# A margin on the ready time in the emitter that interleaves projection pieces with dense matmuls

## The chip, the cores and the metric

The kernel runs on one core of one Trainium2 chip. The metric is the device time of one execution in microseconds. The time of a kernel is the median of its runs; the kernel before was run three times.

## The reference

Two layers of an encoder trunk on 2048 rows of 1024 channels. The even layer runs a gated DeltaNet and an RWKV-7 mixer side by side, the odd layer a Hyena operator. Each begins with one wide input projection. Cut to what matters here:

```python
def even_mixer(x, w_in, ...):
    proj = x @ w_in
    dn_qkv, dn_ab, dn_gate, rk_in, rk_gate = jnp.split(proj, EVEN_SPLITS, axis=-1)
    qkv = jax.nn.silu(dwconv_centred(dn_qkv, dn_conv)).astype(f32)
    q = l2_normalize(q.reshape(bsz, seq, DN_HEADS, DN_DK))
    k = l2_normalize(k.reshape(bsz, seq, DN_HEADS, DN_DK))
    ...
    s = bidir_token_shift(rk_in, rk_mu)
    a = jax.nn.sigmoid(rk_a0 + a_d @ rk_a2)
    kk = l2_normalize(heads(k * rk_k_k))
    k = k * (1.0 + (a - 1.0) * rk_k_a)
    ...

def odd_mixer(x, w_in, ...):
    proj = x @ w_in
    xv, gate = jnp.split(proj, [(HY_ORDER + 1) * HY_WIDTH], axis=-1)
    xv = dwconv_centred(xv, conv_w, conv_b)
    filt = hyena_filters(...)
    ...

def reference(x, p, ...):
    h = x
    for i in range(DEPTH):
        mix = even_mixer(...) if i % 2 == 0 else odd_mixer(...)
        h = layer_norm(DEEPNORM_ALPHA * h + mix @ w_out[i], ln_g[i], ln_b[i])
        e = rms_norm(p[i] @ ple_w[i], ple_norm[i])
        h = h + jax.nn.sigmoid(h @ ple_gate[i]) * e
    return h
```

## The kernel before

The stages run one after another: the even layer's projections (`phase_a`), its two scans, the layer's tail, the odd layer's projections (`phase_d`), the Hyena convolutions, the tail. Both projections are done by `project` (line 1003).

`project` works through a list of jobs. A job is one block of 128 output channels (34 jobs in `phase_a`, 32 in `phase_d`). Its dense part is four blocks, one for each quarter of 512 rows. A block is 24 matmuls of 128x512 into one PSUM bank (8 slices of 128 input channels, and for each the three products of the high and low parts of x and of the weights, `xh`, `xl`, `wh`, `wl`), and ScalarE then copies the bank into the job's row buffer `pb`. There are two such buffers. When all four blocks of a job have been emitted, its four pieces may start, one for each quarter: what happens to these channels behind the projection.

The pieces of `phase_a` come in rounds of eight jobs: `delta(0)` (q), `rwkv(0)`, `delta(1)` (k), a gate, `delta(2)` (v), `rwkv(1)` (k), a gate, `rwkv(2)` (v); there are four rounds behind two small jobs. A piece is a Python generator. It emits some instructions, yields the tile that its next step reads, and goes on when it is chosen again. A `delta` piece for q or k convolves and applies SiLU (`th`, the tile u), and yields it; transposes it on TensorE, copies it to `tm`, squares it on GpSimd (`sq`), and yields that; sums it on VectorE (`ss`, `rs`), raises it to a power on GpSimd (`rr`), and yields that; scales `tm` on VectorE, and yields that; transposes `tm` back on TensorE, copies it out (`cm`) and stores it. The steps from the first transposition on are `normalised` (line 838) and `to_channels`. An `rwkv(1)` piece has one more step, a small matmul with `ad`, before the same normalisation (`kx` in the place of u). A `delta(2)` piece waits once, for u. The pieces of `phase_d` yield no tile, but for those of the filter network `hyena_mlp`, which runs beside them.

The order of emission is made by `weave` (line 1119). Its threads are, in this order, `hyena_mlp` where there is one, four threads of pieces (`post(k)` takes quarter k of every job, one job after another), and `gemm`, which emits the dense blocks. It keeps clocks of the engines by the costs in `Ahead.cost` (line 320) and the time at which each tile is there, `have`. At each turn it takes the first thread whose ready time is not past the clock of TensorE, otherwise the one with the least ready time. After a block `gemm` yields an empty tuple and is ready at once. Before it emits job n, `gemm` yields None, that is, it passes, until all pieces of the jobs up to n-2 are done (`while min(done[:n - 1]) < 4`, line 1096). A yielded tile sets the thread's ready time:

```python
pick = next((t for t in cand if t[1] <= m.clk["P"]), None) or min(cand, key=lambda t: t[1])
m.now = max(pick[1], m.clk["P"])
...
pick[1] = max([m.have.get(x.name, 0.0) for x in r], default=0.0)
```

The scans use `weave` too (line 1687), and then fix the order of every instruction by dependencies of their own. In the projections nothing is fixed: the order of emission is a priority, and the compiler's pass orders each engine's instructions by it and by when it expects their operands.

Of the kernel before, what the change touches and what calls it, by code (L numbers as in the profile page):

```python
# [143 lines left out]
class Ahead:  # L144
# [203 lines left out]
    @staticmethod  # L348
    def beside(out):

        return out.offset // out.ap[0][0] % P >= 64
# [315 lines left out]
class Trunk:  # L667
# [335 lines left out]
    def project(self, src, xh, xl, wp, t2, ps, bank, jobs, pad, beside=None, first=None, tbs=(0, 1, 2, 3), early=None):  # L1003
# [5 lines left out]
        st = {"g": 0}  # L1009

        def fetch(n):
            if n >= NJ:
                return
            r = wp.tile([P, KT, P], F32, name=self.n("wr"), tag="wraw", bufs=1)
            o = 0
            for ap in jobs[n][0]:
                m = ap.shape[1]
                nc.sync.dma_start(r[:, :, o:o + m], ap.rearrange("(k p) m -> p k m", p=P))
                o += m
            raw[n] = r, o  # L1020

        def split(n):
            if n >= NJ:
                return
            r, m = raw.pop(n)
            wh = wp.tile([P, KT, P], F32R, name=self.n("wh"), tag="wh", bufs=2)
            wl = wp.tile([P, KT, P], F32R, name=self.n("wl"), tag="wl", bufs=2)
            nc.scalar.copy(wh[:, :, :m], r[:, :, :m])
            nc.vector.tensor_tensor(wl[:, :, :m], r[:, :, :m], wh[:, :, :m].bitcast(F32), op=ALU.subtract)
            hl[n] = wh, wl, m  # L1030

        def start(n):
            half = jobs[n][1]
            bufs[n] = b = wp.tile([P, T + pad], F32, name=self.n("pb"), tag="pb", bufs=2)
            if half:
                nc.vector.memset(b[:, 0:half], 0.0)
                nc.vector.memset(b[:, half + T:half + T + half], 0.0)

        def block(n, tb):
            wh, wl, m = hl[n]  # L1040
            half = jobs[n][1]
            sl = slice(tb * 512, tb * 512 + 512)
            g = ps.tile([P, 512], F32, name=self.n("g"), tag="gemm", bufs=4)
            k = 0
            for kt in range(KT):
                for a, b in ((wh, xh), (wl, xh), (wh, xl)):
                    nc.tensor.matmul(g[:m, :], a[:, kt, :m], b[:, kt, sl], start=(k == 0), stop=(k == 3 * KT - 1))
                    k += 1
            nc.scalar.copy(bufs[n][:m, half + tb * 512:half + (tb + 1) * 512], g[:m])

        def gemm():
            rows = {}

            tts = [tb * 4 + k for tb in tbs for k in range(4)]

            def row(j, eng=nc.sync):
                if j < NT:
                    tt = tts[j]
                    rows[tt] = [t2("xr"), t2("xr")]
                    for g in range(2):  # L1060
                        eng.dma_start(rows[tt][g], src[tt * P:(tt + 1) * P, g * 512:(g + 1) * 512])

            row(0, early or nc.sync)
            row(1)
            fetch(0)
            for tt in range(2, 5):
                row(tt)
            for n in range(2):
                if n:
                    fetch(n)  # L1070
                split(n)
                start(n)
            for j, tb in enumerate(tbs):
                for k_, tt in enumerate(tts[j * 4:j * 4 + 4]):
                    for g, r in enumerate(rows.pop(tt)):
                        p_ = bank()
                        for q in range(4):
                            nc.tensor.transpose(out=p_[:, q * P:(q + 1) * P], in_=r[:, q * P:(q + 1) * P], identity=self.ident)
                        v = p_.rearrange("p (k t) -> p k t", t=P)
                        h = xh[:, g * 4:g * 4 + 4, tt * P:(tt + 1) * P]  # L1080
                        nc.scalar.copy(h, v)
                        nc.vector.tensor_tensor(xl[:, g * 4:g * 4 + 4, tt * P:(tt + 1) * P], v, h.bitcast(F32), op=ALU.subtract)
                    row(j * 4 + k_ + 5)
                block(0, tb)
                block(1, tb)
                if j == 0 and first:
                    first()
                if j == 1:
                    fetch(2)
                if j == 3:  # L1090
                    split(2)
                    fetch(3)
                yield ()
            st["g"] = 2
            for n in range(2, NJ):
                while min(done[:n - 1]) < 4:
                    yield None
                start(n)
                for tb in range(4):
                    block(n, tb)  # L1100
                    if tb == 1:
                        split(n + 1)
                    if tb == 2:
                        fetch(n + 2)
                    yield ()
                st["g"] = n + 1

        def post(k):
            for i in range(k, 4 * NJ, 4):
                n, q = divmod(i, 4)  # L1110
                while st["g"] <= n:
                    yield None
                yield from jobs[n][2](bufs[n], q)
                done[n] += 1

        self.weave(([beside(st)] if beside else []) + [post(k) for k in range(4)] + [gemm()])


    def weave(self, threads):


        m = self.nc
        live = [[g, 0.0, False] for g in threads]
        idle = 0
        while live:
            cand = [t for t in live if not t[2]]
            if not cand:
                assert idle <= 2 * len(live)
                cand = live
                for t in live:  # L1130
                    t[2] = False
            pick = next((t for t in cand if t[1] <= m.clk["P"]), None) or min(cand, key=lambda t: t[1])
            m.now = max(pick[1], m.clk["P"])
            try:
                r = next(pick[0])
            except StopIteration:
                live.remove(pick)
                r = ()
            if r is None:
                pick[2] = True  # L1140
                idle += 1
                continue
            idle = 0
            pick[1] = max([m.have.get(x.name, 0.0) for x in r], default=0.0)
            for t in live:
                t[2] = False

# [1176 lines left out]
```

## Time and profile before

| | us |
|---|---|
| median of 3 runs | 4395.84 |
| lowest and highest | 4390.16, 4405.48 |
| the profiled execution | 4389.27 |
| its span | 4387.5 |
| even layer's projections in it, with their start | about 0 to 900 |
| odd layer's projections in it | about 2410 to 3140 |

The engines are TensorE (PE; its weight loads PEld), VectorE (DVE), ScalarE (ACT), GpSimd (POOL) and SyncE (SP, which issues the DMAs). A row of a timeline has the start, the duration, the engine, the operation with out<-in, how many were merged, and in brackets the idle time of the engine just before and what ended it. Matmuls overlap: one of 512 columns is shown with 0.39 us, and the next begins 0.23 us after it.

### The profile page before, as it was taken

How to read it: one execution, taken by the hardware profiler on the slowest of the kernel's cores; microseconds unless marked ns; L12 is line 12 of the kernel's file. 1: busy time of each engine (PE TensorE's matmuls, PEld its weight loads, DVE VectorE, ACT ScalarE, POOL GpSimd, SP SyncE). 2: the span in 40 equal slices, each digit the busy share in tenths (PEclk: the TensorE clock that was granted, in tenths of full speed). 3: DMA queues.
4: the chain of work that ended last, by engine and by line, in shares of the span. 5: the costliest groups of instructions: out<-in, count | busy, mean ns of one | idle time of the engine just before them, and what ended most of it. 6: DMA issues, size and time to landing. Idle time of an engine off the chain costs nothing. (4 is left out here: it accounts for less than half of the span.)

```text
span 4387.5 us, 86695 instructions
## 1 busy us (share of the span) xinstructions
PE 4192.0 (96%) x34638; PEld 3553.6 (81%) x34638; DVE 2782.6 (63%) x4505; ACT 2305.7 (53%) x4501; POOL 1739.4 (40%) x1609
## 2 busy tenths in 40 slices
PE   8999999989999999979999999999899999988999
PEld 6877777768888888867887888888789999977887
DVE  5555555568888899975443444344388888875443
ACT  5334333357777777753222333233489999963222
POOL 0121211245555788763332000000277877853333
PEclk9999999989999999999999999999999999999999
DMA  3233323253334444434212311111302021114211
GB/s 117 72 92 87 90 76 89 68 159 117 118 117 142 124 146 147 145 96 160 68 63 69 104 64 57 64 67 65 121 23 61 24 71 42 33 49 171 68 63 45
DMA packets 381340, 389.99 MB, mean 89 GB/s; under 512 B 111706, under 2 KB 300865, under 8 KB 372489
## 3 DMA queue, kind: packets, MB, share of 16 engines
q1 hardware_dynamic: 379785, 380.78, 28.2%
q8 instruction: 273, 4.47, 0.4%
q10 hardware_dynamic: 1152, 3.67, 0.2%
q14 instruction: 130, 1.06, 0.1%
HBM read 264.23 MB, written 120.13 MB: 88 GB/s over the span
## 5 line engine op out<-in xcount | busy, mean ns | idle before, releaser
L162 ACT COPY pb<-g 128x512 f32<-128x512 f32 (+1 forms) x264 | 155.3, 588 | 856.2 <-PE g L162 853.6
L162 PE MATMUL g<-xh,wh 128*128 128x512 f32 (+1 forms) x1088 | 431.6, 397 | 0.1
L162 PE MATMUL g<-xh,wl 128*128 128x512 f32 (+1 forms) x1088 | 427.8, 393 | 0.3 <-DVE wl L162 0.3
L162 PE MATMUL g<-xl,wh 128*128 128x512 f32 (+1 forms) x1088 | 426.9, 393 | 0.0
L162 PE MATMUL g<-hh,wh 128*128 128x512 f32 x1024 | 402.7, 393 | 0.5 <-ACT hh L162 0.2
L162 PE MATMUL g<-hl,wh 128*128 128x512 f32 x1024 | 398.5, 390 | 0.0
L162 PE MATMUL g<-hh,wl 128*128 128x512 f32 x1024 | 398.4, 389 | 0.0
L162 DVE SCALAR_TENSOR_TENSOR cv<-pb,pc,cv 128x512 f32<-128x512 f32 (+1 forms) x304 | 225.8, 750 | 168.1 <-ACT pb L162 87.7
L661 POOL MEMSET grain.4059_32437<- 64x2048 f32 x1 | 1.8, 1802 | 734.9 <-PE g L162 734.9
L162 PEld LDWEIGHTS g<-xh,wh 128*128 128x128 f32 (+1 forms) x1088 | 205.0, 188 | 47.3 <-issue 3.7
L162 PEld LDWEIGHTS g<-xl,wh 128*128 128x128 f32 (+1 forms) x1088 | 204.6, 188 | 44.6 <-DVE xl L162 0.3
L162 PEld LDWEIGHTS g<-xh,wl 128*128 128x128 f32 (+1 forms) x1088 | 204.6, 188 | 43.9 <-DVE wl L162 0.7
L162 POOL TENSOR_TENSOR sq<-tm 128x512 f32<-128x512 f32 x48 | 51.9, 1092 | 469.1 <-ACT tm L162 469.1
L162 PEld LDWEIGHTS g<-hh,wh 128*128 128x128 f32 x1024 | 192.2, 188 | 45.9 <-ACT pb L162 3.2
L162 PEld LDWEIGHTS g<-hh,wl 128*128 128x128 f32 x1024 | 192.2, 188 | 41.4 <-issue 1.9
L162 PEld LDWEIGHTS g<-hl,wh 128*128 128x128 f32 x1024 | 192.2, 188 | 40.4 <-DVE hl L162 0.3
L162 ACT CAST h<-sp 128x512 fp32r<-128x512 f32 (+1 forms) x96 | 46.2, 514 | 313.8 <-PE sp L162 313.8
L162 POOL TENSOR_TENSOR yl<-y,yh 128x1024 fp32r<-128x1024 f32 x30 | 73.6, 2453 | 296.7 <-ACT yh L162 296.7
L162 DVE SCALAR_TENSOR_TENSOR u<-u,tg 128x512 f32<-128x512 f32 x64 | 43.8, 687 | 231.2 <-PE tg L162 231.2
L162 DVE SCALAR_TENSOR_TENSOR pm<-pb,hcol,a 128x512 f32<-128x512 f32 x64 | 73.2, 1153 | 135.2 <-ACT pb L162 134.7
L162 DVE SCALAR_TENSOR_TENSOR a<-pb,hcol,a 128x512 f32<-128x512 f32 x128 | 94.2, 742 | 99.4 <-ACT pb L162 60.5
L162 ACT ACTIVATE tg<-tg 128x512 f32<-128x512 f32 x64 | 37.2, 582 | 207.2 <-PE tg L162 207.2
(767 smaller groups left out, 13138.9 us busy)
## 6 DMA issues: line engine op xcount, KB each, us to landing
grain.45_7042<-s_rk SPq DMA_DIRECT2D x32, 1024.0 KB
wr<-in_even_w_in SPq DMA_DIRECT2D x33, 512.0 KB
wr<-in_odd_w_in SPq DMA_DIRECT2D x32, 512.0 KB
y<-s_y SPq DMA_DIRECT2D x30, 512.0 KB
xr<-in_x SPq DMA_DIRECT2D x32, 256.0 KB
s_qk<-cm SPq DMA_DIRECT2D x32, 256.0 KB
s_kv<-tm SPq DMA_DIRECT2D x32, 256.0 KB
s_gate<-th SPq DMA_DIRECT2D x32, 256.0 KB
```

The source lines that it names most:

```text
L162: f(*a, **kw)
L661: r = f(*map(bare, a), **{k: bare(x) for k, x in kw.items()})
```

## The change

`weave` gets a second argument, `spare`, with 0.0 as the value where none is given. `project` passes 4.0. The ready time of a thread that has yielded tiles is then the latest time of those tiles plus `spare`, in the microseconds of the emitter's own clocks. A thread that yields an empty tuple stays ready at once. The time of the tiles themselves, `have`, and the clocks are not changed. The scans' call of `weave` has no `spare`.

```diff
-        self.weave(([beside(st)] if beside else []) + [post(k) for k in range(4)] + [gemm()])
+        self.weave(([beside(st)] if beside else []) + [post(k) for k in range(4)] + [gemm()], 4.0)
...
-    def weave(self, threads):
+    def weave(self, threads, spare=0.0):
...
-            pick[1] = max([m.have.get(x.name, 0.0) for x in r], default=0.0)
+            pick[1] = max([m.have.get(x.name, 0.0) + spare for x in r], default=0.0)
```

## Rows read from the trace of the kernel before

**Rows 1.** The page: busy time and share of each engine, number of instructions.
```profile
PE 4192.0 (96%) x34638; PEld 3553.6 (81%) x34638; DVE 2782.6 (63%) x4505; ACT 2305.7 (53%) x4501; POOL 1739.4 (40%) x1609
```

**Rows 2.** Windows: stretch, length, busy by engine, granted clock, DMA share, GB/s.
```profile
66.00:900.00 834.00, 804.55 (x3695) 652.32 (x3695) 462.27 (x696) 323.47 (x533) 160.96 (x129) 0.99 0.32 82
...
2410.00:3140.00 730.00, 727.64 (x3224) 594.07 (x3224) 305.56 (x436) 237.66 (x343) 0.47 (x1) 1.00 0.20 69
```

**Rows 3.** Waits of PE, 66 to 900 us: total us, times, longest us.
```profile
PE tr L162 <- DVE tm L162: 27.2, 16, 3.6
PE tr L162 <- DVE th L162: 2.2, 1, 2.2
```

**Rows 4.** Timeline of PE, 121 to 137 us, a `delta(0)` job's transposes.
```profile
121.27 1.03 PE L162 MATMUL tr<-ident,th 128*128 128x128 f32 x8
...
127.64 1.04 PE L162 MATMUL tr<-ident,th 128*128 128x128 f32 x8
128.51 1.04 PE L162 MATMUL tr<-ident,tm 128*128 128x128 f32 x8
129.30 0.48 PE L162 MATMUL g<-xh,wh 128*128 128x512 f32 x1
...
132.83 0.39 PE L162 MATMUL g<-xh,wh 128*128 128x512 f32 x1
134.69 0.63 PE L162 MATMUL tr<-ident,tm 128*128 128x128 f32 x4 [1.47 <-DVE tm L162]
...
136.77 0.60 PE L162 MATMUL tr<-ident,tm 128*128 128x128 f32 x4
```

**Rows 5.** Timeline of DVE and POOL, 128 to 134 us, and another `wl` at 156.
```profile
128.99 1.04 POOL L162 TENSOR_TENSOR sq<-tm 128x512 f32<-128x512 f32 x1 [1.43 <-ACT tm L162]
...
130.67 1.88 DVE L162 TENSOR_TENSOR wl<-wr,wh 128x1024 fp32r<-128x1024 f32 x1
...
132.77 1.01 POOL L162 TENSOR_TENSOR rr<-rs,mhalf 128x4 f32<-128x4 f32 x1 [1.30 <-DVE rs L162]
...
133.86 0.68 DVE L162 TENSOR_TENSOR tm<-tm,rr 128x512 f32<-128x512 f32 x1
...
156.07 1.22 DVE L162 TENSOR_TENSOR wl<-wr,wh 128x1024 fp32r<-128x1024 f32 x1
```

**Rows 6.** Timeline of PE, 184 to 186 us, a `delta(1)` job's last transposes.
```profile
184.07 0.63 PE L162 MATMUL tr<-ident,tm 128*128 128x128 f32 x4 [1.36 <-DVE tm L162]
185.07 0.63 PE L162 MATMUL tr<-ident,tm 128*128 128x128 f32 x4 [0.36 <-DVE tm L162]
```

**Rows 7.** Timeline of PE, POOL and DVE, 254 to 260 us, the end of `rwkv(1)`.
```profile
254.41 1.47 PE L162 MATMUL tr<-ident,tm 128*128 128x128 f32 x12
...
255.96 1.63 POOL L162 TENSOR_TENSOR rr<-rs,mhalf 128x8 f32<-128x8 f32 x1 [1.49 <-DVE rs L162]
257.63 1.75 DVE L162 TENSOR_TENSOR tm<-tm,rr 128x512 f32<-128x512 f32 x1 [1.81 <-POOL rr L162]
259.43 0.66 PE L162 MATMUL tr<-ident,tm 128*128 128x128 f32 x4 [3.55 <-DVE tm L162]
```

**Rows 8.** Windows after waits; columns as in Rows 2, the granted clock third from last.
```profile
260.00:262.00 2.00, 2.00 (x11) 1.64 (x11) 2.00 (x3) 1.11 (x2) 1.54 (x2) 1.00 0.12 36
...
463.00:465.00 2.00, 1.80 (x7) 1.61 (x8) 2.00 (x3) 0.60 (x2) 1.54 (x2) 0.50 0.00 0
465.00:467.00 2.00, 2.00 (x8) 1.62 (x7) 2.00 (x2) 0.64 (x3) 1.83 (x1) 0.74 0.76 192
...
668.00:670.00 2.00, 1.67 (x6) 1.58 (x7) 2.00 (x3) 0.47 (x1) 1.54 (x2) 0.50 0.00 0
670.00:672.00 2.00, 2.00 (x6) 1.52 (x6) 2.00 (x2) 0.65 (x3) 1.96 (x1) 0.50 0.69 179
672.00:680.00 8.00, 8.00 (x32) 6.49 (x31) 5.22 (x10) 1.94 (x3) 1.59 (x1) 0.86 1.01 251
...
875.00:878.00 3.00, 3.00 (x11) 2.47 (x12) 3.00 (x3) 1.10 (x2) 2.57 (x3) 0.61 0.29 77
...
130.00:140.00 10.00, 8.53 (x43) 6.79 (x42) 9.59 (x15) 7.11 (x14) 3.39 (x4) 1.00 0.74 205
```

## The prediction

> **What bounds the kernel now.** I read the page first, then the busy time by stage, then TensorE's waits in the stage that the change touches, then its instructions in order of time. The page has PE busy for 96% of the span [rows 1]: the kernel is a queue of matmuls, and time is won or lost only where PE stands idle or runs at the lower clock. Two stages go through `project`. In the odd layer's (2410 to 3140 us) PE is busy 727.64 of 730 us at a granted clock of 1.00, so nothing is left to win there [rows 2]. In the even layer's, PE is busy 804.55 of 834 us from 66 us on [rows 2]. The 29.4 us that are missing are nearly all one wait: 27.2 us, in 16 pieces, on DVE for the normalised tile `tm`; 2.2 us more are one wait on `th` in the first job [rows 3]. That is all that an order of emission can win back.
>
> The 16 waits repeat in each of the four rounds of eight jobs: one of about 1.5 us in the first `delta` job (134.69 us; the others are at 338, 544 and 750 us), a pair of 1.36 and 0.36 us in the second (184.07 and 185.07 us), and one of 3.55 us in the `rwkv(1)` job (259.43 us) [rows 4, 6, 7]. A round has 6.8 us of them, four rounds 27.2 us, the sum of the waits. All are transposes that fetch `tm` back to channel order, the last step of a piece.
>
> The order that runs is not quite the order that is emitted. In rows 4 the reader is to see that a group of four `tm` transposes stands in the middle of a dense block: the block begins at 129.30 us, 16 of its 24 matmuls run, 0.2267 us apart, to the one at 132.83, and then come the transposes. Emission by `weave` never cuts a block. So what `weave` emits first is a priority, and the compiler's own pass moves a transpose that it thinks not ready behind matmuls that are. Where that pass is too hopeful, PE waits: here the last step came from DVE only at 133.86 plus 0.68 us [rows 5].
>
> **The change part by part.** No instruction is added or removed: the same matmuls, transposes, copies, POOL squares and powers, and the same DMAs. What moves is the moment at which a piece's next step is emitted: a step waiting on `u`, `sq`, `rr` or `tm` counts as ready 4.0 us of `weave`'s own clock later. Steps that yield `()` stay ready at once, because the maximum of an empty list stays 0.0.
>
> First, the steps that cannot move. `gemm` may not emit job n before all four pieces of job n-2 are done (line 1096). When the four blocks of job n-1 are out, nothing but pieces is left, and `weave` then takes the piece with the smallest ready time whether it is ready or not. The same margin on every piece leaves that order nearly unchanged. The waits of 1.5, 1.36, 0.36 and 3.55 us are of this kind: in rows 4, 6 and 7 they stand behind the last block of the next job. So the margin does not give the stalled transposes any slack; what it intends happens only to steps that already had some.
>
> Second, the steps that move. In a `delta` job the `th` transposes of the first two quarters now come after the third block (121.27 us, eight in a row) and those of the other two after the fourth (127.64 us, with the `tm` of the first two behind them) [rows 4]. By the emitter's own arithmetic in `cost`, which decides the order and is no time of the chip, the first quarter's `th` has been ready for 3.997 units when it is taken (198.37 against a PE clock of 202.36), so with 4.0 it just misses and comes a block later; the second had 0.29 and misses too. All four quarters then go through copy, square, sum, power and scaling side by side after the fourth block, and all four `tm` groups are forced steps, where today two are. This holds for eight jobs (`q` and `k` in four rounds); the four `v` jobs have no `tm` and only lose an earlier transposition, which nothing on PE follows: zero, hidden by the next block, about 24 x 0.2267 = 5.4 us.
>
> What the two extra forced groups cost is not in the trace of before; I bound it by the nearest rows. From below: the first group takes the wait that the third takes today, the other three follow at no cost, as the second does at 136.77 us: 0. Below nothing too: if the weight split `wl` that stands between sum and power (1.88 us; 1.22 us elsewhere) [rows 5] falls behind the four chains instead of between them, the 1.5 us shrink by at most the 1.88 us, so by all of it: -1.5 us a job. From above: the wait of `rwkv(1)`, the one job in which four quarters already go through POOL together, is 3.55 us [rows 7], which is 1.9 us more than the 1.47 to 1.72 us of a `delta` job. Between these, the four powers pass POOL one after another, 1.01 us each [rows 5], and the pair at 184.07 and 185.07 us shows 0.36 us of wait for one such successor [rows 6]. I take this row, the nearest: three successors instead of one, 2 x 0.36 = 0.7, and 0.3 for the two more squares (1.04 us each) [rows 5] ahead of the first power, an estimate from the same share: **+1.0 us a job, +8 us for eight**. Ends: -12 and +15 us.
>
> In `rwkv(1)` the steps on `cv`, `kx` and `sq` move a block or so, the second half of its chain moves towards the forced end, and the twelve transposes at 254.41 us, which did not wait, come with the four that did [rows 7]. The last power (255.96, 1.63 us) and the last scaling (257.63, 1.75 us) were already back to back on POOL and DVE [rows 7], and a later start of the chain puts matmuls of the next job in front of them. I take 0, with ends of -3.5 (the wait gone) and +1.5 us a job (one more `delta`-sized wait): -14 to +6 us.
>
> Third, the clock. After the 3.55 us of idle the granted clock was 0.50 from 463 to 465 and 0.74 to 467 us (1.5 us lost), 0.50 from 668 to 672 and 0.86 to 680 us (3.1 us lost), 0.61 from 875 to 878 us (1.2 us lost); after the same wait at 259 us it stayed 1.00, and after the waits of 1.5 us too [rows 8]. So 5.8 us are lost, and four short waits in place of one long one would give some of it back. I take -2, with ends of -6 and +4 us. The Trainium skill (TensorE: Matmul & The Clock Gate, section Why this matters for your kernels) would have every long gap between bursts of matmuls fall back to the lower level; the trace agrees in three of four rounds only. By that rule the four gaps cost the same each, and closing all of them would be worth a little more than the rows say.
>
> In the odd layer only the filter network's pieces yield a tile; they have a free priority on a PE that is never idle: 0, hidden by the dense matmuls (727.64 of 730 us) [rows 2]. If that cover were gone, 16 steps would cost up to a block each; nothing shows that.
>
> The sum: +8 + 0 - 2 = **+6 us**. The profiled execution took 4389.27 us (span 4387.5 us), so it would take 4395; the median of the three runs shown is 4395.84 us, 6.6 us above it, so I forecast **4402 us**.
>
> **The rivals.** *Faster.* The margin may do what it says: the pass places a transpose where the chain really ends, and the long waits close. All of it would be 27.2 us of waits and 5.8 us of clock, down to 4363 us; half of it, -17 us, gives 4379. For it speaks that every wait sits on a step whose model was too early; against it, that these very steps are forced, and the margin doesn't delay a forced step. It decides from -13 us, half of the waits.
>
> *Slower.* The second pair of quarters makes the chain on POOL as long as in `rwkv(1)`: each of the eight `delta` jobs pays that job's 3.55 us instead of 1.5 to 1.7 (+15 us), `rwkv(1)` gets one more short wait (+6 us): +21, 4417 us. It decides from 1.7 us a job on. For it speaks that the four squares and four powers need POOL for 8.2 us where a block of dense work is 5.4 us; against it, that a dense block of the next job but one is there as filler, and the pass knows most of the chain.
>
> *The change does nothing.* The pass sorts both emissions into the same order on PE: 4396 us. The two orders differ in which block a transposition follows, and a block can't be passed by a step emitted after it unless its matmuls wait, so I hold this for unlikely.
>
> **How the numbers follow.** What a measurement of this kernel can tell from no change is about 0.3%, 13 us. Forecast and the rival without effect, both within it: 0.62 (0.57 and 0.05). Slower: 0.23. Faster: 0.15. The range goes from -12 us (4384) to +24 us (4420), that is through most of the slower case and up to the point at which the faster one decides.
>
> **What would show it.** Right, step by step: in the profile after, the `th` transposes of a `delta` job stand in one group of 16 behind the fourth block; four `tm` groups stand inside the next job's first block; the waits of PE on `tm` are in more than 16 pieces and sum to 27 to 40 us; the odd layer's stage is as long as before to within 2 us. Wrong: waits on `tm` below 14 us, or a group of `th` still behind the third block, or a wait of PE in this stage on a new releaser (the `t2k` buffers, the copies from PSUM on ACT).

## The result, and the profile after

| | before | after |
|---|---|---|
| median, us (4 runs each, same chip) | 4400.1 | 4428.52 |
| lowest and highest | 4390.16, 4405.48 | 4427.93, 4433.69 |
| profiled execution, its span | 4389.27, 4387.5 | 4428.9, 4427.1 |
| end of the even layer's projections in it | 904.18 | 938.72 |
| idle time of PE from 66 us to there | 29.5 | 46.5 |
| time lost to the clock in the same stretch | 8.8 | 30.8 |

The ratio is 1.0073 (95% interval 1.0059 to 1.0087): 0.73% slower, outside the range that I gave. The end of the stage is that of its last PE instruction. The time lost to the clock is summed over windows of 2 us, (1 - granted clock) x 2 us each.

The profiled execution of before is 10.8 us faster than the median of its runs, so the two spans differ by 39.6 us where the medians differ by 28.4. Of the 39.6 us, 34.5 lie in the even layer's projections: 17.0 of idle, and 17.5 in which PE is busy for longer. The second part goes with the 22.0 us of lost clock, which are more because a stretch at the lower clock may hold idle time too. The odd layer's dense work takes 722.8 us against 723.5 before, from its first `g` matmul to its last. The rest lies in stages whose order the change doesn't touch.

The page after has PE busy for 20.9 us more than [rows 1], with the same number of instructions: the extra goes with matmuls that run at the lower clock. It is followed by the window of the whole stage and one of the odd layer's (columns as in [rows 2], the granted clock third from last; the first window ends 38.72 us later than that of [rows 2]).

```profile
PE 4212.9 (95%) x34638; PEld 3572.2 (81%) x34638; DVE 2783.7 (63%) x4505; ACT 2303.2 (52%) x4501; POOL 1742.7 (39%) x1609
...
66.00:938.72 872.72, 826.25 (x3705) 668.66 (x3704) 468.08 (x700) 325.51 (x536) 164.69 (x129) 0.96 0.31 79
...
2500.00:3180.00 680.00, 679.67 (x2988) 555.68 (x2987) 285.98 (x409) 217.76 (x310) 0.00 (x0) 1.00 0.18 61
```

The waits of PE in the stage after (total us, times, longest) answer to [rows 3]:

```profile
PE tr L162 <- DVE rs L162: 24.9, 8, 3.1
PE tr L162 <- DVE tm L162: 15.8, 12, 1.8
PE tr L162 <- ACT th L162: 3.1, 4, 1.1
PE tr L162 <- DVE th L162: 2.7, 1, 2.7
```

The first line is new: one wait of about 3.1 us in each of the eight `delta` jobs for q and k, which had 13.0 us of waits together before. (It is shown under `rs`; the waiting transposes read `tm`, and `rs` is a last short step of DVE beside it.) The next two lines are the four `rwkv(1)` jobs: 18.9 us where there were 4 x 3.55 = 14.2. Here is the first `delta` job after, PE, POOL and DVE from 126 to 141 us; it answers to [rows 4, 5]:

```profile
126.95 1.91 PE L162 MATMUL tr<-ident,th 128*128 128x128 f32 x16
128.30 1.04 POOL L162 TENSOR_TENSOR sq<-tm 128x512 f32<-128x512 f32 x1 [127.86 <-ACT tm L162]
128.61 0.48 PE L162 MATMUL g<-xh,wh 128*128 128x512 f32 x1
...
129.73 3.02 POOL L162 TENSOR_TENSOR sq<-tm 128x512 f32<-128x512 f32 x2 [0.39 <-ACT tm L162]
129.98 1.87 DVE L162 TENSOR_TENSOR wl<-wr,wh 128x1024 fp32r<-128x1024 f32 x1
...
131.77 1.00 DVE L162 TENSOR_SCALAR rs<-ss 128x4 f32<-128x4 f32 x1
...
132.15 0.39 PE L162 MATMUL g<-xh,wh 128*128 128x512 f32 x1
...
132.85 1.03 POOL L162 TENSOR_TENSOR rr<-rs,mhalf 128x4 f32<-128x4 f32 x1
133.85 1.07 POOL L162 TENSOR_TENSOR sq<-tm 128x512 f32<-128x512 f32 x1
...
133.94 1.53 DVE L162 TENSOR_TENSOR tm<-tm,rr 128x512 f32<-128x512 f32 x1
135.62 0.63 PE L162 MATMUL tr<-ident,tm 128*128 128x128 f32 x4 [3.09 <-DVE rs L162]
...
136.96 0.63 PE L162 MATMUL g<-xh,wl 128*128 128x512 f32 x1
137.38 1.91 PE L162 MATMUL tr<-ident,tm 128*128 128x128 f32 x8
...
139.52 0.82 PE L162 MATMUL tr<-ident,tm 128*128 128x128 f32 x4
```

All 16 `th` transposes stand in one group behind the fourth block, and all four `tm` groups inside the next one, the first behind 16 of its matmuls. So the order moved as forecast. The first group waits 3.09 us instead of 1.47. What covers its chain on PE is no shorter: from the start of the last group of `th` transposes to the wait there are 16 transposes and 16 matmuls in both kernels. The chain is longer, by the whole 1.62 us: it begins 0.69 us earlier (the square of the waiting quarter at 128.30 us instead of 128.99) and its scaling ends 0.93 us later. Two steps of VectorE take up the difference, each beside squares on POOL:

- `rs`, which stands behind `wl`, takes 1.00 us instead of 0.16, as it does in all eight `delta` jobs for q and k. It ends at 132.77 us; the squares of the second and third quarter end at 132.75. Its row before:

```profile
132.47 0.16 DVE L162 TENSOR_SCALAR rs<-ss 128x4 f32<-128x4 f32 x1
```

- The scaling takes 1.53 us instead of 0.68, since POOL squares the fourth quarter beside it (133.85 to 134.92 us). The Trainium skill (SBUF — State Buffer, section SBUF: two separate sides) says that VectorE, where it reads two inputs, and GpSimd exclude each other for a whole instruction; by that rule the scaling would end 0.68 us behind the square, at 135.60 us, and the trace has 135.47. In three of the eight jobs the scaling takes 0.68 us, and another quarter's `rs`, of 1.02 us, stands in front of it.

The other three groups wait for nothing. But the matmuls behind the wait take 0.63 us instead of 0.39: the clock has fallen. Windows after the first two of these waits, and of the four waits in the first `rwkv(1)` job, answer to [rows 8]:

```profile
134.00:136.00 2.00, 0.38 (x4) 0.41 (x5) 2.00 (x4) 0.00 (x0) 2.00 (x2) 1.00 0.56 168
136.00:138.00 2.00, 2.00 (x10) 1.57 (x9) 1.56 (x4) 1.21 (x2) 2.00 (x3) 0.64 0.06 17
138.00:140.00 2.00, 2.00 (x11) 1.75 (x10) 1.67 (x4) 1.53 (x3) 0.31 (x1) 0.51 0.41 115
...
188.00:190.00 2.00, 2.00 (x8) 1.71 (x7) 1.57 (x4) 1.12 (x2) 2.00 (x3) 0.50 0.46 131
190.00:192.00 2.00, 2.00 (x12) 1.74 (x11) 1.31 (x3) 0.68 (x2) 0.36 (x1) 0.71 0.84 234
...
264.00:266.00 2.00, 0.23 (x2) 0.15 (x2) 1.73 (x2) 0.58 (x1) 2.00 (x3) 1.00 0.00 0
266.00:268.00 2.00, 2.00 (x8) 1.71 (x8) 2.00 (x3) 1.10 (x2) 0.92 (x1) 0.56 0.01 4
268.00:270.00 2.00, 2.00 (x6) 1.53 (x6) 0.42 (x3) 0.00 (x0) 1.43 (x1) 0.58 0.87 183
```

In the first window PE is busy for 0.38 of 2 us at full clock, and in the next two it is busy all the time at 0.64 and 0.51. The level 0.50 is 1.2 GHz, 1.00 is 2.4. By job, from the waits and from such windows over the whole stage:

| us | idle before | idle after | lost clock before | lost clock after |
|---|---|---|---|---|
| first job (`th`) | 2.2 | 2.7 | 1.7 | 3.4 |
| eight `delta` jobs | 13.0 | 24.9 | 0 | 17.0 |
| four `rwkv(1)` jobs | 14.2 | 18.9 | 6.8 | 10.2 |

The largest single term is the clock in the `delta` jobs: each lost 1.7 us, two of them 3.4, where no `delta` job had lost anything. And this is the `rwkv(1)` job that lost its single wait of 3.55 us [rows 7] for four shorter ones (PE, 261 to 273 us):

```profile
261.83 0.66 PE L162 MATMUL tr<-ident,tm 128*128 128x128 f32 x4 [1.35 <-DVE tm L162]
...
263.42 0.66 PE L162 MATMUL tr<-ident,tm 128*128 128x128 f32 x4 [0.94 <-DVE tm L162]
...
265.85 0.77 PE L162 MATMUL tr<-ident,tm 128*128 128x128 f32 x4 [1.77 <-DVE tm L162]
...
272.15 0.63 PE L162 MATMUL tr<-ident,tm 128*128 128x128 f32 x4 [1.06 <-ACT th L162]
```

The twelve transposes that had followed without a wait at 254.41 us now wait too: 5.1 us in this job.

### The profile page after: what moved, and what is told of

Same layout as the page of the kernel before. It is cut to its first block, busy times and chain, and to the rows that moved or that the text cites. A ratio compares the mean times of both kernels' runs of the same rounds, so it can differ in the third digit from the quotient of the medians.

```text
span 4427.1 us, 86663 instructions
## 1 busy us (share of the span) xinstructions
PE 4212.9 (95%) x34638; PEld 3572.2 (81%) x34638; DVE 2783.7 (63%) x4505; ACT 2303.2 (52%) x4501; POOL 1742.7 (39%) x1609
## 5 line engine op out<-in xcount | busy, mean ns | idle before, releaser
L162 DVE TENSOR_TENSOR wl<-wr,wh 128x1024 fp32r<-128x1024 f32 (+1 forms) x66 | 86.8, 1316 | 123.4 <-ACT wh L162 123.2
```

Of the source, the lines that this page charges most:

```text
L162: f(*a, **kw)
```

## The experiments

The ratios are to the kernel before, with 95% intervals; stage end, idle time and lost clock are taken as above. No kernel leaves out work. "Squares on ScalarE" is a change to `normalised` that is explained with e8.

| run | ratio | stage end | idle | lost clock |
|---|---|---|---|---|
| after | 1.0073 (1.0059 to 1.0087) | 938.72 | 46.5 | 30.8 |
| e1 margin in the `delta` jobs | 1.0046 (1.0028 to 1.0063) | 927.43 | 42.9 | 20.5 |
| e2 margin in the `rwkv` jobs | 1.0030 (1.0021 to 1.0039) | 916.55 | 37.7 | 18.8 |
| e3 margin in the odd layer | 1.0002 (0.9993 to 1.0012) | 908.25 | 29.9 | 15.4 |
| e4 margin on the wait for `th` | 1.0055 (1.0040 to 1.0070) | 927.92 | 42.3 | 21.0 |
| e7 margin 3.99 | 1.0049 (1.0033 to 1.0064) | 928.80 | 38.0 | 29.0 |
| e5 no forced steps, no margin | 0.9907 (0.9886 to 0.9929) | 864.78 | 0.5 | 0.3 |
| e6 no forced steps, margin 4 | 0.9973 (0.9963 to 0.9984) | 893.34 | 18.5 | 12.2 |
| e8 squares on ScalarE, margin 4 | 1.0018 (1.0008 to 1.0028) | 917.13 | 33.3 | 17.1 |
| e9 squares on ScalarE, no margin | 0.9945 (0.9931 to 0.9960) | 881.99 | 14.0 | 2.1 |
| e10 as e9, no forced steps | 0.9912 (0.9895 to 0.9928) | 865.15 | 1.4 | 0.0 |
| e11 as e9, margin in `delta` jobs | 0.9972 (0.9962 to 0.9983) | 894.17 | 22.0 | 3.4 |
| e12 as e9, margin in `rwkv` jobs | 1.0013 (1.0004 to 1.0022) | 914.34 | 34.3 | 20.5 |

### Which jobs: e1, e2, e3

In the even layer, `post` sets the margin by the job's place in its round (e2 has `in (1, 5, 7)`, the `rwkv` jobs), and `weave` reads it; e3 keeps the margin of the change for the odd layer's call alone.

```diff
-                yield from jobs[n][2](bufs[n], q)
+                for r in jobs[n][2](bufs[n], q):
+                    self.spare = 4.0 if pad == 4 and n > 1 and (n - 2) % 8 in (0, 2, 4) else 0.0
+                    yield r
...
-            pick[1] = max([m.have.get(x.name, 0.0) + spare for x in r], default=0.0)
+            pick[1] = max([m.have.get(x.name, 0.0) + self.spare for x in r], default=0.0)
```

> The margin of 4.0 only on the pieces of the delta jobs (q, k, v) of the even layer; every other piece and the odd layer as before. Theory A (the bunching of four quarters in the delta jobs makes one longer wait in each q and k job, and the clock falls after it): eight waits of about 3.1 us where there were 1.5 to 1.7, so +11 us of idle, and some 2 us of lost clock behind each, +14 us or so: 0.5 to 0.65% slower than before, 4420 to 4428. Theory B (it is the rwkv(1) chain that is pushed out): within 0.15% of before. Theory C (the odd layer's filter network): no change.

> The margin only on the pieces of the rwkv jobs of the even layer. Theory A: four rounds with waits of 4 to 5.1 us in pieces where there was one of 3.55 us: +3 to +6 us of idle and about as much lost clock, 0.1 to 0.25% slower than before. Theory B: nearly the whole loss, 0.5 to 0.75% slower. Theory C: no change.

> The margin only in the odd layer's projections. Theories A and B: same time as before within 0.1%, because PE has no idle time there. Theory C: most of the 0.73%.

Waits of PE in the stage, e1 and then e2:

```profile
PE tr L162 <- DVE rs L162: 24.9, 8, 3.1
PE tr L162 <- DVE tm L162: 14.6, 5, 3.6
...
PE tr L162 <- DVE tm L162: 35.0, 28, 2.4
```

e1 has the eight waits of 3.1 us and keeps the 3.55 us of `rwkv(1)`. e2 has the short waits of before in the `delta` jobs, and 22.0 us (35.0 less 13.0) in the four `rwkv(1)` jobs instead of 14.2. The losses, 0.46% and 0.30%, add up to the whole; the `delta` jobs carry three fifths of it. The first is a little under what I had expected of theory A, the second above that of theory A and under that of theory B. The odd layer carries nothing: 0.02%, with zero in its interval. e3 is also a measure of the noise: its even stage has the order and the waits of before (27.2 us in 16 pieces), and lost 15.4 us to the clock where before lost 8.8. A single execution's lost clock is good to some 7 us, and the step from about 9 to 15 up to 31 is above that.

### Which step of the delta jobs: e4, e7

e4 gives the margin to the wait for `th` alone, e7 makes it 3.99, just under the 3.997 by which the first quarter's `th` is late in the emitter's own account.

```diff
-            pick[1] = max([m.have.get(x.name, 0.0) + spare for x in r], default=0.0)
+            pick[1] = max([m.have.get(x.name, 0.0) + (spare if x.name.startswith("th_") else 0.0) for x in r], default=0.0)
```

> The margin only on the first wait of a piece that yields th (the delta jobs' u, and the small first job); the waits on sq, rr and tm and all of the rwkv pieces as before. Theory A in its sharp form (only the first transposes move, the later steps are forced whatever the margin): the same time as with the margin on all steps of the delta jobs, to within 0.1%, and one wait of about 3.1 us in each q and k job. If the margin on the later steps matters too: less than half of that loss.

> The change with 3.99 in the place of 4.0, which is just under the 3.997 by which the first quarter's th of every delta job is late: that one step goes back to behind the third block, all else stays as with 4.0. Theory A (the long wait comes from the first quarter's chain starting behind the fourth block with nothing ready in front of it): the first tm group stands ready behind the fourth block, the wait of 3.1 us falls to 1.3 to 1.9 us in the eight q and k jobs and no clock is lost there; what is left is the rwkv(1) part: 0.25 to 0.4% slower than before, 4406 to 4413. Rival (bunching any three quarters is enough, or the margin as such costs): still 0.6% or more slower.

e4 has the same two lines of waits as e1, to the digit, and ends the stage within 0.5 us of it. Its loss is within 0.1% of e1's, as the sharp form of theory A had it. The margin on the steps behind it (`sq`, `rr`, `tm`) does nothing in these jobs, which fits the prediction's first step: they are forced. The loss there comes from one decision, the `th` transposes of the first two quarters emitted behind the fourth block instead of the third.

In e7 the first quarter's transposes go back behind the third block; three quarters are still processed side by side. Its first `delta` job (`rs`, scaling and wait), its waits in the stage, and its windows there:

```profile
130.95 1.00 DVE L162 TENSOR_SCALAR rs<-ss 128x4 f32<-128x4 f32 x1
133.12 0.68 DVE L162 TENSOR_TENSOR tm<-tm,rr 128x512 f32<-128x512 f32 x1
133.95 1.09 PE L162 MATMUL tr<-ident,tm 128*128 128x128 f32 x4 [2.27 <-DVE rs L162]
...
PE tr L162 <- DVE rs L162: 18.0, 8, 2.3
...
132.00:134.00 2.00, 0.05 (x1) 0.08 (x2) 2.00 (x6) 0.00 (x0) 1.66 (x2) 0.97 0.82 198
134.00:136.00 2.00, 2.00 (x7) 1.81 (x8) 1.83 (x3) 0.93 (x2) 1.65 (x2) 0.50 0.66 195
136.00:138.00 2.00, 2.00 (x9) 1.61 (x9) 1.74 (x4) 1.24 (x3) 0.00 (x0) 0.68 0.72 199
```

The wait is 2.27 us where I had expected 1.3 to 1.9, and all eight still brought the clock down: the loss of 0.49% lies between theory A (0.25 to 0.4%) and the rival (0.6% or more). The scaling is back at 0.68 us here and `rs` is not, and the wait is 0.80 us above the 1.47 of before. Three quarters at once still cost 18.0 us of wait against 24.9 for four, and the threshold at 3.997 decides only over 0.24% (1.0073 against 1.0049).

### Whether the waits sit on forced steps: e5, e6

e5 (from the kernel before) and e6 (from the kernel after) let `gemm` emit job n when all pieces of the jobs up to n-2 have begun, where both kernels want them done. A piece has begun when its first step that emits something is out.

```diff
-                while min(done[:n - 1]) < 4:
+                while min(begun[:n - 1]) < 4:
...
-                yield from jobs[n][2](bufs[n], q)
+                first = True
+                for r in jobs[n][2](bufs[n], q):
+                    if first and r is not None:
+                        begun[n] += 1
+                        first = False
+                    yield r
```

> The kernel before, without margin, but the dense part of job n waits only until the pieces of job n-2 have begun (their convolution is emitted, the only reader of the row buffer), not until they are done. Theory (the waits sit on steps that are forced out before their operands can be there): no tm group inside a block any more, PE's waits on tm nearly gone (under 5 us of 27), the clock stays up, 0.6 to 0.8% faster than before, 4360 to 4370. Rival (the waits come from too optimistic a pass wherever a step stands, or the freed order runs into the buffers of the pieces): within 0.3% of before.

> The same release of the dense part with the margin of 4.0. Theory: with nothing forced, the margin only moves steps later that were not waiting; the waits stay small and the time is that of the same kernel without margin to within 0.3%, unless the pieces, now up to three jobs behind, run out of their 14 row tiles: then PE waits on ACT or on stores and some of the gain is lost. Rival (the margin costs by itself): 0.5% or more slower than without it.

The stage of e5 (window to its end, then all its waits):

```profile
66.00:864.78 798.78, 798.31 (x3713) 648.87 (x3712) 462.55 (x701) 322.85 (x537) 158.04 (x129) 1.00 0.33 86
...
PE tr L162 <- DVE th L162: 0.2, 1, 0.2
PE tr L162 <- DVE tm L162: 0.2, 1, 0.2
```

Next to nothing waits, the clock stays up, and the stage is 39.4 us shorter than before. So the waits of before went with the gate on `done`, and e5 beats both kernels, by 0.93% the one before, more than the theory had. With the margin on top (e6) 0.66% of this goes again, as the rival had it, by a wait that none of the kernels so far has and by the clock behind it (12.2 us); here are the waits in the stage, and the first of them:

```profile
PE tr L162 <- DVE cv L162: 16.7, 5, 6.1
...
279.44 1.09 PE L162 MATMUL tr<-ident,cv 128*128 128x128 f32 x4 [3.50 <-DVE cv L162]
```

The transposes of `rwkv(2)`'s convolution (`cv`) wait for DVE, which is busy with the last steps of `rwkv(1)` and with the gate's. Where nothing is forced, the margin doesn't add slack for free either: it moves the wait to another tile.

### What the POOL squares have to do with it: e8, e9, e10, e11, e12

The scaling took 1.53 us beside a POOL square. These kernels square on ScalarE; e8 and e9 are the kernels after and before with this edit, e10, e11 and e12 are e5, e1 and e2 with it.

```diff
-                nc.gpsimd.tensor_tensor(sq, tm, tm, op=ALU.mult)
+                nc.scalar.activation(sq, tm, AF.Square)
```

> The change with the square of tm on ScalarE in the place of GpSimd (in delta and rwkv(1) pieces). Theory A with contention (the first scaling took 1.53 us and not 0.69 because GpSimd was squaring the fourth quarter, and the squares hold up the powers): the first scaling takes 0.7 us, wl 1.2 us, the wait of the first tm group falls from 3.1 to about 1.5 us, the clock stays up, and the time is within 0.3% of before. Rival (the wait is the pass's estimate of the chain, whatever the engine): the wait stays at 2.5 us or more and the time at 0.5% or more above before.

> The kernel before, without margin, with the square of tm on ScalarE. It separates what the square's engine does by itself from what it does for the margin. Theory (the square on GpSimd lengthens the chain only where four quarters are bunched): the waits on tm fall little, from 27 to between 18 and 27 us, and the time is 0 to 0.3% below before; the margin then costs, on this base, 0.2 to 0.4% in place of 0.73%, nearly all of it in rwkv(1). Rival (the square's engine is a gain of its own): 0.5% or more below before, and the margin costs as much as on the old base.

> The kernel whose dense part waits only until pieces have begun, without margin, and with the square on ScalarE. Theory (where no step is forced and PE waits for nothing, the length of the chain doesn't matter): within 0.15% of the same kernel with the square on GpSimd, 4345 to 4362, 0.8 to 1.1% below before. Rival (chains still set the time): a further 0.3% or more below.

> The margin only on the delta pieces, with the square on ScalarE. Theory (in the delta jobs the square on GpSimd is what makes the bunched chain long enough for a wait of 3.1 us and the lost clock behind it): against the kernel without margin and the same square (0.9945 of before), 0.1 to 0.25% more, that is 0.9955 to 0.997 of before; waits of about 1.2 us and no lost clock in the q and k jobs. Rival (bunching costs the same whatever the square's engine): 0.46% more, 0.999 of before.

> The margin only on the rwkv pieces, with the square on ScalarE. Theory (with the square moved, nearly all of the margin's cost is the rwkv(1) chain that starts a block later, with waits of about 2 us and the clock lost behind them): against the same square without margin 0.45 to 0.65% more, 0.999 to 1.001 of before. Rival (rwkv(1) costs what it did on the old base): 0.3% more, 0.9975 of before.

First e9, its waits, and the end of an `rwkv(1)` job:

```profile
PE tr L162 <- DVE tm L162: 11.7, 12, 1.2
...
255.01 0.63 PE L162 MATMUL tr<-ident,tm 128*128 128x128 f32 x4 [0.51 <-DVE tm L162]
```

The edit by itself wins 0.55%, as the rival to my theory had it: the 3.55 us of `rwkv(1)` shrink to 0.51, and apart from the stage's first microseconds no clock is lost. The square takes 0.64 us on ScalarE instead of 1.04, and the scaling 692 ns on the average instead of 915 (48 of them). So the effect of the edit must be taken against e9, not against before.

Then e8, the first `delta` job (power to transposes), and a wait in `rwkv(1)` with its windows:

```profile
133.68 0.69 DVE L162 TENSOR_TENSOR tm<-tm,rr 128x512 f32<-128x512 f32 x1 [1.02 <-POOL rr L162]
134.51 0.63 PE L162 MATMUL tr<-ident,tm 128*128 128x128 f32 x4 [1.15 <-DVE tm L162]
...
261.55 1.09 PE L162 MATMUL tr<-ident,tm 128*128 128x128 f32 x4 [2.01 <-DVE tm L162]
...
260.00:262.00 2.00, 0.45 (x3) 0.48 (x3) 2.00 (x2) 0.31 (x1) 2.00 (x2) 0.64 0.00 0
262.00:264.00 2.00, 2.00 (x7) 1.71 (x7) 2.00 (x3) 1.33 (x3) 0.53 (x1) 0.50 0.00 0
```

With the scaling at 0.69 us and no `rs` held up, the bunched `delta` job waits 1.15 us instead of 3.09, again behind 16 `th` transposes in one group and 16 matmuls, and no `delta` job loses the clock. In e9, where nothing is bunched, this wait is 1.22 us: without squares on POOL, bunching doesn't lengthen it. Taken against e9, the margin still costs 0.73% (1.0018 against 0.9945), where I had expected 0.2 to 0.4%, but shared out otherwise: the `delta` jobs 0.27% (e11 against e9), the `rwkv` jobs 0.68% (e12). Together these are more than the whole: `rwkv(1)` waits for 5.4 to 5.9 us a round in e12 and for 3.8 us in e8, so the two interact, and no run shows how. So on the kernel as it is the long wait of the `delta` jobs, and the clock behind it, need the POOL squares beside DVE. The 0.27% stay without them: of the 12.2 us by which e11's stage is longer than e9's, 8.0 are idle time, most of it short waits of the later groups (0.4 to 0.9 us). The `rwkv` part doesn't need the squares. That it comes from the later start of the chain fits e2 and e12, and no run tests it apart. e10 shows the other side: where nothing is forced, the engine of the squares makes no difference that the intervals can tell (0.9912 and 0.9907).

## Why the prediction was wrong

**What bounds the kernel** held. PE is the queue, the waits on forced transposes are what can be won in the stage, and e5 won them: 39.4 us there, against the 33 that I had read from waits and clock (27.2 + 5.8). The clock's part was 6.8, as my windows cut each of the three low stretches short, and the first job's 2.2 us of wait and 1.7 of clock come on top.

**First, the steps that can't move** held: e4 and e1 have the same waits to the digit, so the margin gives the stalled steps of the `delta` jobs nothing.

**Second, the `delta` jobs**: the order was right in each point (one group of 16, four groups in the next block, no wait for the last three). The size was not: +11.9 us of idle against +8, inside the ends of -12 to +15. I had set the first group's wait at today's value and added a share of 0.3 us for the squares; these cost it 0.84 us through an `rs` of 1.00 instead of 0.16 us and 0.85 us through a scaling of 1.53 instead of 0.68. The 0.7 us for three successors did not come: the other groups wait for nothing. I had counted the squares as time on POOL ahead of the power, and not what a square does to DVE beside it, though [rows 5, 7] had a scaling of 0.68 us in one place and 1.75 in another, and `wl` of 1.88 and 1.22. The waits on `tm` came to 43.8 us in 24 pieces, above the 27 to 40 that I had named as a sign of being right.

**`rwkv(1)`** was mis-sized too: +4.7 us against 0, inside the ends of -14 to +6, by the mechanism that I named for the upper one.

**Third, the clock, is the step that failed**: -2 us forecast, with ends of -6 and +4, and +22.0 measured (+17.5 as busy time of PE; +15.4 lost if e3, whose even stage has the order of before, is the base). With the idle time alone the kernel would have stayed within my range. I let the clock follow the waits of 3.55 us that became shorter, and didn't ask it of the `delta` waits that became longer, although my own upper end for them was that same 3.55 us. Between 1.5 us, where [rows 8] show a clock of 1.00, and 3.55 us, where they show falls, I had no row, and took the price of a longer wait to be its length. The trace of before had one: the first job's wait of 2.2 us [rows 3] ends at 83.67 us, and PE goes on at the lower clock:

```profile
84.00:86.00 2.00, 2.00 (x7) 1.58 (x7) 2.00 (x4) 1.98 (x4) 0.00 (x0) 0.50 0.07 12
```

Counted over the runs, with every wait of PE in the stage from 1.1 us on, but for one of 1.84 us in e11 that no fall followed; a fall comes during the wait or up to 1.3 us behind it:

| waits of | in | with a fall of the clock |
|---|---|---|
| 1.15 to 1.22 us (`delta`, alone or with 0.4 to 0.9 behind) | e8, e9, e11, e12 | 0 of 32 |
| 1.36 to 1.56 us (`delta`, alone or with 0.36 behind) | before, e2, e3 | 1 of 24 |
| 2.21 to 2.74 us (first job's `th`) | all but e5, e6, e10 | 10 of 11 |
| 2.24 to 2.27 us (`delta`) | e7 | 8 of 8 |
| 3.08 to 3.14 us (`delta`) | after, e1, e4 | 22 of 24 |
| 3.55 us (`rwkv(1)`) | before, e1, e3, e4 | 14 of 16 |
| 3.50 to 6.08 us (`rwkv(2)`'s `cv`) | e6 | 4 of 4 |
| two to four in a row, 3.8 to 5.9 us together (`rwkv(1)`) | after, e2, e7, e8, e12 | 20 of 20 |

A `delta` job thus paid 1.5 us of idle and 2.1 us (17.0 / 8) of clock for its longer wait. The Trainium skill (TensorE: Matmul & The Clock Gate, section Why this matters for your kernels) would have each long gap fall back to the lower level. I had weighed that rule only against the four gaps of before and read it as worth little; three of those four agreed with it, and the change made eight more such gaps. The four short waits of `rwkv(1)`, which I thought would spare the clock, brought it down each time, before the fourth of them: PE was busy for 1.94 of the 6 us ahead of the fall at 266 us.

**The rivals.** The slower one is the nearest, but only in part by its own mechanism: four quarters at once do lengthen the chain, to a wait of about 3.1 us a `delta` job (I said 3.55), and `rwkv(1)` waits longer. But the power did not stand in POOL's queue (it begins 0.08 us behind `rs`); the squares held up two steps of VectorE. The idle time grew by 1.5 us a `delta` job, under the 1.7 from which this rival was to decide, and the clock, which it left out, carries half of the stage's loss. The faster rival and the one without effect are out: no wait closed, and the order moved.

**What is open.** The clock's part was read from rows of every run, and no kernel kept a wait and changed the clock alone. Why 4 of the 40 `delta` and `rwkv(1)` waits above 3 us kept the full clock isn't settled. Nor is the rest of the difference between the two profiled spans, 5 us behind the stage: lost clock in the scans differs between the executions (18.8 and 23.9 us from 1000 to 2300 us), and no run took it apart.

## What to carry to other kernels

When an edit lengthens a wait of the matmul engine, price it twice: once for its length, and once for the clock behind it, by the rows of the nearest wait that brought the clock down; a wait 1.5 us longer cost 3.6 us here. A margin on ready times can't help a step that a gate forces: find the gate first (here on `done`, where `begun` is enough), since taking it away won 0.93%, more than any other edit here. Steps that one bunches also meet on the engines beside the bound one: a step of the chain took twice its time there, and a short one six times.

## What the runs showed of the hardware

- The clock fell with single waits of 2.21 us and more in 58 of the table's 63 cases, with waits of 1.15 to 1.56 us in 1 of 56, and with two to four waits in a row in 20 of 20. A fall with a single `delta` wait of 2.24 us or more cost 1.7 us of clock in 28 of 30 cases and 3.4 in two; one with waits in a row cost 3.4 or 5.1 us in 18 of 20.
- A VectorE `TENSOR_TENSOR` of 128x512 f32 took 0.68 us without a GpSimd square beside it and 1.53 us with one; a `TENSOR_SCALAR` of 128x4 took 0.16 and 1.00. The square of 128x512 took 1.04 us alone, and two of them took 3.02 us beside a `TENSOR_TENSOR` of 128x1024: both sides pay.
- ScalarE squares 128x512 in 0.64 us; moving these squares there is worth 0.55% of this kernel by itself, but nothing on top of e5.
